# Down projection of an encoder: seven block products dealt anew over three phases, sums made in place

## The chip, the cores and the metric

The kernel runs on one core of a Trainium2 chip. A core has TensorE (PE: matrix products; PEld is its loading of weights), VectorE (DVE), ScalarE (ACT), GpSimd (POOL) and SyncE (SP, which here issues the DMAs). The metric is the device time of one execution in microseconds, lower is better; the time before is the median of three executions.

## The reference, cut to what matters

Two layers, 512 tokens, width 1024, all in float32. Each layer ends with the feed-forward part:

```python
h = rms_norm(x, pre_ffn_norm[l])
gate, up = jnp.split(jnp.einsum('bsd,df->bsf', h, ffn_w_gate_up[l]), 2, axis=-1)   # df: 2 x 2816
f = jnp.einsum('bsf,fd->bsd', jax.nn.silu(gate) * up, ffn_w_down[l])               # 2816 -> 1024
x = x + rms_norm(f, post_ffn_norm[l])
```

The change lies in the second product, f, which is called the down stage here.

## The kernel before

**Precision.** A float32 product is made of three: each operand is split into a high half (`A.activation(hi, src, Copy)`, written as fp32r by ACT) and a low half (`src - hi`, a subtraction on DVE or POOL), and `mm3` issues high by high, low by high, high by low into one PSUM bank. So each operand of the down stage costs one ACT and one DVE/POOL instruction of its width before PE can use it.

**The down stage (`down`).** The 2816 rows of the weight are 22 tiles of 128; tile k and tile k+11 are the two halves of the inner dimension (H = 11). Activations `act[k]` (a1) and `act[k+11]` (a2) are 128 x 512: columns q0 (tokens 0 to 255) and q1 (256 to 511). Weights are 128 x 1024: columns c0 and c1. With the blocks A11, A12 / A21, A22 of the activations and B11, B12 / B21, B22 of the weight, the 2 x 2 block product is made with seven products (a Strassen-Winograd form), each 11 steps of k with two banks (j = 0, 1) and three 128 x 512 matmuls in each: 66 matmuls.

- Phase 1 (`span(at, at + 56)`): four products m1, m5, m6, m7, 24 matmuls for each k. The names of PSUM are `ps_tp` (m1), `ps_mm` (m5), `ps_sc` (m6), `ps_av` and `ps_mm` (m7).
- Phase 2 (`span(at + 57, at + 85)`): two products, m2 and m3, in `ps_tp` and `ps_sc`, 12 matmuls for each k.
- Phase 3 (`span(at + 85, at + 99)`): one product m4 in `ps_mm`, 6 matmuls for each k, while the sums of the others are evacuated, normed and added to x (`post_half`, `finish`). In layer 0 `finish` also norms for the next layer and transposes (`ps_tp<-ident,p`).

Before, phase 1 reads tile k whole (r1, in `raw` or `tab`) and the right half of tile k+11 straight into `carry[k]`, which lies in the buffers `hT_h` and `hT_l`. Those hold the normed input that gate/up multiplies by, so they come free when gate/up's last product has read them. The sums of the Strassen form are made with subtractions (`sub(VG, ...)`) into `tmp`, `s`, `raw`, `carry` and `act`; VG lets the planner choose DVE or POOL.

**Gate/up (`ffn`)** makes act[f] for f = 0 to 21, from f = 2 on also in a Strassen form (`strassen`); the half act[f][:, 256:512] is written by POOL in the trace (`stk<-v` or `mix<-v`). One f takes PE 10.0 us.

**The order of the work.** The program records all operations, and `Program.run` plans them by a list: each has a priority by its place in the spans, costs and delays from a table in the code, and the planner writes one fixed order for each engine. An engine takes its instructions in that order; an instruction that waits holds up all behind it. Buffers: `raw` 2, `tab` 2, `whi` and `wlo` 4 each, `p` 3, `pT` 2, `s` 3, `tmp` 2, `stk` 18, `mix` 8. In layer 0 the norm weights of the next layer hold one of the two `tab` from phase 2 on. Every instruction has the one line L447 in the trace (L448 after), so tiles tell them apart. A split of weights reads `whi<-raw` on ACT and `wlo<-raw,whi` on DVE; one of activations `p<-stk` and `pT<-stk,p`.

Of the kernel before, what the change touches and what calls it, by code (L numbers as in the profile page):

```python
# [452 lines left out]
def encoder_kernel(  # L453
# [564 lines left out]
    def ffn(l, hT, at):  # L1018
# [120 lines left out]
        return act  # L1139

    def down(l, act, at):

# [54 lines left out]

        with pr.span(at + 56, at + 57):
            w1 = load_norm(l, 3, "v2")
            w2 = None if last else load_norm(l + 1, 0)  # L1200
# [4 lines left out]
            for j in range(2):
                u1, u2, u3, u5 = part_c[j]
                V.tensor_tensor(u3, m7[j], u2, ALU.add)
                V.tensor_tensor(u5, m5[j], u3, ALU.add)
                V.tensor_tensor(u2, m5[j], u2, ALU.add)
        with pr.span(at + 57, at + 85):  # L1210
            m2, m3 = ([bank(t), bank(t)] for t in ("tp", "sc"))
            for k in range(H):
# [8 lines left out]
                prod(m2, a, 0, w, c0, k)
                prod(m3, a, 256, w, c1, k)
        with pr.span(at + 85, at + 99):
            if not last:
# [4 lines left out]
            for j in range(2):
                u1, u2, u3, u5 = part_c[j]  # L1230
                for h, u, m in ((0, u1, m2[j]), (1, u2, m3[j])):
                    V.tensor_tensor(u, m, u, ALU.add)
                    post_half(ss[j], h, u, w1, u)
                finish(j, (u1, u2))
            tail = []
            for k in range(H):
                a1, a2 = act[k], act[k + H]
                w, a = (T("whi", F32R), T("wlo", F32R)), T("mix", F32R)
                a = a[:, q0], a[:, q1]
                split(w[0][:, c0], w[1][:, c0], a1, e=VG)  # L1240
                split(*a, a2[:, q1], e=VG)
                if k < H - 2:
                    prod(m4, a, 0, w, c0, k)
                else:
                    tail.append((a, w, k))
            for j in range(2):
# [2 lines left out]
                u3, u5 = part_c[j][2:]
                sub(V, u3, u3, m4[j])  # L1250
                post_half(ss[2 + j], 0, u3, w1, u3)
                finish(2 + j, (u3, u5))
# [117 lines left out]
```

## Time and profile before

| | us |
|---|---|
| median of 3 executions | 1298.52 (1298.27 to 1300.25) |
| profiled execution, its own time | 1296.75 |
| span of the trace | 1295.0 |
| PE busy / DVE busy / ACT busy / POOL busy in the span | 1230.5 / 1102.0 / 765.2 / 246.7 |
[...]

In a row of the timeline the numbers are start and duration in us, and in brackets the idle time of that engine just before and what ended it. Durations of neighbours overlap a little, so the price of an instruction in a full queue is the distance of two starts. A row of busy times by stretch reads: stretch, its length, busy us (and instructions) of PE, PEld, DVE, ACT and POOL, granted clock, DMA share, GB/s. Stretches used below: in layer 0 phase 1 runs from the end of gate/up at 523.49 to 592.79, phase 2 to 625.65, phase 3 to 650.58; in layer 1 from 1162.33 to 1231.51, 1265.91 and 1285.43, and the program ends 9.57 us later.

### The profile page before, as it was taken

The numbers are of one execution on the slowest core, as the hardware profiler recorded it, in microseconds if no ns is written. First come the engines' busy times: TensorE is split into PE (matmuls) and PEld (weight loads), VectorE is DVE, ScalarE is ACT, GpSimd is POOL, SyncE is SP. The second block draws the span as 40 slices with busy tenths as digits, with TensorE's granted clock in tenths as the row PEclk, the third lists the DMA queues.
The fourth block names the chain that finished last, engine by engine and source line by source line (L and its number), as shares of the span: only waits on it lengthen the run. The fifth ranks groups of instructions, "written<-read, shape, count | busy, mean of one in ns | idle before, by whom it ended". The sixth has DMA issues, their size and how long they took to land.

```text
span 1295.0 us, 20878 instructions
## 1 busy us (share of the span) xinstructions
PE 1230.5 (95%) x7608; PEld 1082.3 (84%) x7608; DVE 1102.0 (85%) x2147; ACT 765.2 (59%) x1515; POOL 246.7 (19%) x314
## 2 busy tenths in 40 slices
PE   7999999999999999999899999999999999998896
PEld 5787887888999999767677878878799999996674
DVE  5688889869888888999868797897798888889987
ACT  4675779755554455555646675796455544455553
POOL 1334423011011111001214353220201111110011
PEclk9999899999999999999899998999999999999999
DMA  6341232112333323524233321321233233325231
GB/s 223 113 144 60 70 100 80 33 50 98 114 98 113 116 99 98 175 80 138 72 112 121 121 70 50 111 62 50 67 98 113 98 100 119 109 84 185 77 119 66
DMA packets 42247, 129.68 MB, mean 100 GB/s; under 512 B 6048, under 2 KB 7072, under 8 KB 42144
## 3 DMA queue, kind: packets, MB, share of 16 engines
q1 hardware_dynamic: 42144, 128.35, 30.4%
q8 instruction: 60, 0.98, 0.3%
q14 instruction: 43, 0.35, 0.1%
HBM read 120.98 MB, written 2.10 MB: 95 GB/s over the span
## 4 chain that ended last, share of the span: by engine, by line
PE 69%; DVE 21%; ACT 3%; issue 3%; DMA 3%; POOL 1%; SPq 0%; DVEq 0%; POOLq 0%; ACTq 0%
PE ps_mm L447 39%; PE ps_sc L447 18%; PE ps_tp L447 9%; DVE wlo L447 6%; PE ps_av L447 4%; DVE pT L447 3%; DVE stk L447 2%; DVE v L447 2%; DVE tmp L447 1%; DVE s L447 1%; DMA raw<-in_wdn_dram 1%; ACT stk L447 1%; DVE tab L447 1%; ACT p L447 1%; DVE xs L447 1%
## 5 line engine op out<-in xcount | busy, mean ns | idle before, releaser
L447 ACT ACTIVATE whi<-raw 128x1024 fp32r<-128x1024 f32 (+2 forms) x186 | 180.2, 987 | 54.3 <-DMA raw<-in_wdn_dram 18.7
L447 DVE TENSOR_TENSOR wlo<-raw,whi 128x1024 fp32r<-128x1024 f32 (+2 forms) x171 | 192.1, 1139 | 19.9 <-ACT whi L447 19.2
L447 PE MATMUL ps_mm<-hT_h,whi 128*128 128x256 f32 (+1 forms) x352 | 114.6, 326 | 0.0
L447 PE MATMUL ps_mm<-hT_l,whi 128*128 128x256 f32 (+1 forms) x352 | 113.6, 323 | 0.3 <-DVE hT_l L447 0.3
L447 PE MATMUL ps_mm<-hT_h,wlo 128*128 128x256 f32 (+1 forms) x352 | 113.8, 323 | 0.1
L447 POOL TENSOR_TENSOR cb<-cb,mhalf 128x1 f32<-128x1 f32 (+3 forms) x52 | 54.5, 1052 | 237.0 <-DVE cb L447 234.5
L447 PE MATMUL ps_tp<-ident,p 128*128 128x128 f32 x608 | 87.2, 283 | 11.8 <-DVE p L447 11.7
L447 POOL TENSOR_TENSOR stk<-v 128x256 f32<-128x256 f32 x32 | 37.8, 1182 | 304.9 <-ACT v L447 264.4
L447 PE MATMUL ps_sc<-stk,stk 96*128 96x512 f32 (+2 forms) x320 | 92.6, 387 | 3.4 <-ACT p L447 2.5
L447 PEld LDWEIGHTS ps_tp<-ident,p 128*128 128x128 f32 x608 | 73.6, 146 | 22.4 <-DVE p L447 11.2
L447 DVE TENSOR_TENSOR pT<-ps_tp,pT 128x512 fp32r<-128x512 f32 (+1 forms) x128 | 79.0, 650 | 12.2 <-ACT pT L447 11.5
L447 ACT ACTIVATE pT<-ps_tp 128x512 fp32r<-128x512 f32 (+1 forms) x128 | 67.0, 567 | 26.7 <-PE ps_tp L447 25.8
L447 PE MATMUL ps_av<-pT,v 128*128 128x256 f32 x480 | 76.6, 289 | 6.1 <-DVE mix L447 3.5
L447 PEld LDWEIGHTS ps_av<-pT,v 128*128 128x128 f32 x480 | 69.1, 190 | 15.3 <-ACT pT L447 5.3
L447 ACT ACTIVATE v<-ps_mm 128x256 f32<-128x256 f32 (+3 forms) x72 | 26.6, 382 | 86.0 <-PE ps_mm L447 85.5
L447 PE MATMUL ps_mm<-whi,hT_h 128*128 128x512 f32 (+1 forms) x176 | 70.8, 402 | 1.5 <-DVE stk L447 1.0
L447 PEld LDWEIGHTS ps_mm<-hT_l,whi 128*128 128x128 f32 x352 | 66.4, 189 | 6.2 <-DVE hT_l L447 0.5
L447 PEld LDWEIGHTS ps_mm<-hT_h,wlo 128*128 128x128 f32 x352 | 66.5, 189 | 5.2 <-DVE wlo L447 0.3
L447 PEld LDWEIGHTS ps_mm<-hT_h,whi 128*128 128x128 f32 x352 | 66.5, 189 | 4.5
L447 PEld LDWEIGHTS ps_sc<-stk,stk 96*128 96x128 f32 (+2 forms) x320 | 52.3, 194 | 21.4 <-ACT p L447 5.3
L447 PE MATMUL ps_sc<-v,p 128*128 128x256 f32 x320 | 69.5, 280 | 0.0
L447 PE MATMUL ps_sc<-hT_h,wlo 128*128 128x256 f32 x224 | 64.4, 288 | 4.7 <-POOL wlo L447 4.7
(253 smaller groups left out, 3982.5 us busy)
## 6 DMA issues: line engine op xcount, KB each, us to landing
raw<-in_wgu_dram SPq DMA_DIRECT2D x48, 512.0 KB, 4.4
tab<-in_wgu_dram SPq DMA_DIRECT2D x40, 512.0 KB, 3.5
raw<-in_wdn_dram SPq DMA_DIRECT2D x28, 512.0 KB, 3.6
raw<-in_win_f_dram SPq DMA_DIRECT2D x16, 512.0 KB, 3.5
raw<-in_wo_dram SPq DMA_DIRECT2D x16, 512.0 KB, 3.5
tab<-in_wdn_dram SPq DMA_DIRECT2D x16, 512.0 KB, 3.4
raw<-in_win_g_dram SPq DMA_DIRECT2D x8, 512.0 KB, 3.7
tab<-in_natab_dram SPq DMA_DIRECT2D x8, 512.0 KB, 3.4
```

Of the source, the lines that this page charges most:

```text
L447: o.ins = getattr(self.issue[o.eng], method)(*[real(v) for v in a], **{k: real(v) for k, v in kw.items()}).ins
```

## The change

The seven products are kept, with other operands and in another distribution: phase 1 makes m1, m5, m6 and m2, phase 2 makes m7 and m3, phase 3 m4. Phase 1 reads both weight tiles whole, r1 into `raw` and r2 into `tab`, makes its sums in place in them and splits each 1024 wide; B of the last product is written to `carry[k]` as a plain difference, which nobody reads before phase 3. One sum of activations is made at the end of each gate/up step f >= 11, in place in act[f - 11], by two 256-wide operations. Phase 2 reads the two right halves again, as two loads of 256 KB, and makes one weight sum and two activation sums.

```diff
@@ ffn, after strassen(f)
+                if f >= H:
+                    a1, a2 = act[f - H], act[f]
+                    VG.tensor_tensor(a1[:, t1], a1[:, t1], a2[:, t1], ALU.add)
+                    VG.tensor_tensor(a1[:, t1], a1[:, t1], a1[:, t0], ALU.subtract)
@@ down, phase 1
-            m1, m5, m6 = ([bank(t), bank(t)] for t in ("tp", "mm", "sc"))
-            m7 = [bank("av"), bank("mm")]
+            m1, m6, m5 = ([bank(t), bank(t)] for t in ("tp", "sc", "mm"))
+            m2 = [bank("av"), bank("mm")]
             for k in range(H):
-                a1, a2, b22 = act[k], act[k + H], carry[k]
-                r1 = T(("raw", "raw", "tab", "tab")[k % 4])
+                a1, a2 = act[k], act[k + H]
+                r1, r2 = T("raw"), T("tab")
                 SP.dma_start(r1, wdn[l, k])
-                SP.dma_start(b22, wdn[l, k + H][:, c1])
-                t1, d = T("tmp"), T("s")
-                sub(VG, t1, r1[:, c1], r1[:, c0])
-                sub(VG, r1[:, c1], b22, r1[:, c1])
-                sub(VG, b22, b22, t1)
-                sub(VG, d[:, q0], a1[:, q0], a1[:, q1])
-                VG.tensor_tensor(d[:, q1], a1[:, q1], a2[:, q1], ALU.add)
-                sub(VG, a1[:, q1], d[:, q1], a1[:, q0])
+                SP.dma_start(r2, wdn[l, k + H])
+                d = T("s")[:, q0]
+                sub(VG, r1[:, c1], r1[:, c1], r1[:, c0])
+                sub(VG, r2[:, c1], r2[:, c1], r1[:, c1])
+                VG.tensor_tensor(d, a1[:, q1], a1[:, q0], ALU.add)
                 a = T("p", F32R), T("pT", F32R)
                 wa, wb = ((T("whi", F32R), T("wlo", F32R)) for _ in range(2))
-                for o, c, src in ((a, c0, a1), (wa, c0, r1[:, c0]), (a, c1, d), (wa, c1, t1), (wb, c0, b22),
-                                  (wb, c1, r1[:, c1])):
-                    split(o[0][:, c], o[1][:, c], src, e=VG)
-                sub(VG, a1[:, q0], a2[:, q0], a1[:, q1])
+                split(*wa, r1, e=VG)
+                split(a[0][:, 0:512], a[1][:, 0:512], a1, e=VG)
+                split(a[0][:, 512:768], a[1][:, 512:768], d, e=VG)
+                split(*wb, r2, e=VG)
+                split(a[0][:, 768:], a[1][:, 768:], a2[:, q0], e=VG)
+                sub(VG, carry[k], r2[:, c1], r2[:, c0])
...
@@ down, phase 2
-                r = T(("raw", "raw", "tab")[k % 3])
-                SP.dma_start(r, wdn[l, k + H])
+                r = T(("raw", "tab")[k % 2])
+                SP.dma_start(r[:, c0], wdn[l, k][:, c1])
+                SP.dma_start(r[:, c1], wdn[l, k + H][:, c1])
+                sub(VG, r[:, c0], r[:, c1], r[:, c0])
+                sub(VG, a2[:, q0], a2[:, q0], a1[:, q1])
+                sub(VG, a1[:, q1], a2[:, q1], a1[:, q1])
                 w, a = (T("whi", F32R), T("wlo", F32R)), (T("p", F32R), T("pT", F32R))
                 split(*w, r, e=VG)
-                split(a[0][:, q0], a[1][:, q0], a2[:, q0], e=VG)
-                split(a[0][:, q1], a[1][:, q1], a1[:, q0], e=VG)
-                sub(VG, a1, carry[k], r[:, c0])
+                split(a[0][:, q0], a[1][:, q0], a1[:, q1], e=VG)
+                split(a[0][:, q1], a[1][:, q1], a2[:, q0], e=VG)
...
```

The evacuation after phase 1 has five DVE operations where it had eight; the one after phase 2 has six where it had four.

What the planner makes of it on DVE, at three places. First, one steady step of phase 1 in layer 0. Before, twelve of the thirteen instructions of a step (a 128 x 512 `tmp<-tab` stands ahead of them):

```order
L447 TENSOR_TENSOR s_6700<-stk_4599 128x256
L447 TENSOR_TENSOR tab_6552<-hT_h_6431,tab_6552 128x512
L447 TENSOR_TENSOR s_6700<-stk_4599,stk_5952 128x256
L447 TENSOR_TENSOR hT_h_6431<-hT_h_6431,tmp_6693 128x512
L447 TENSOR_TENSOR stk_4599<-s_6700,stk_4599 128x256
L447 TENSOR_TENSOR wlo_6721<-tab_6552,whi_6640 128x512
L447 TENSOR_TENSOR pT_6727<-s_6700,p_6714 128x512
L447 TENSOR_TENSOR pT_6727<-stk_4599,p_6714 128x512
L447 TENSOR_TENSOR wlo_6721<-tmp_6693,whi_6640 128x512
L447 TENSOR_TENSOR wlo_6734<-hT_h_6431,whi_6711 128x512
L447 TENSOR_TENSOR wlo_6734<-tab_6552,whi_6711 128x512
L447 TENSOR_TENSOR stk_4599<-stk_5952,stk_4599 128x256
```

After, the whole step (raw is r1, tab is r2, the last row writes carry):

```order
L448 TENSOR_TENSOR raw_6610<-raw_6610 128x512
L448 TENSOR_TENSOR s_6680<-stk_4599 128x256
L448 TENSOR_TENSOR tab_6624<-tab_6624,raw_6610 128x512
L448 TENSOR_TENSOR pT_6688<-stk_4599,p_6629 128x512
L448 TENSOR_TENSOR wlo_6694<-raw_6610,whi_6685 128x1024
L448 TENSOR_TENSOR pT_6688<-s_6680,p_6629 128x256
L448 TENSOR_TENSOR wlo_6708<-tab_6624,whi_6696 128x1024
L448 TENSOR_TENSOR pT_6688<-stk_5964,p_6629 128x256
L448 TENSOR_TENSOR hT_h_6463<-tab_6624 128x512
```

Nine instructions stand where thirteen stood; four narrow splits of weights are two wide ones.

Second, phase 2 of layer 0 on DVE. Before, from one weight sum for phase 3 (`stk<-hT_h,raw`) to the next split but one:

```order
L447 TENSOR_TENSOR stk_4240<-hT_h_6431,raw_7031 128x512
L447 TENSOR_TENSOR wlo_7091<-raw_7050,whi_7080 128x1024
L447 TENSOR_TENSOR pT_7104<-stk_5706,p_7070 128x256
L447 TENSOR_TENSOR pT_7104<-stk_4365,p_7070 128x256
L447 TENSOR_TENSOR v_6968<-v_6968,v_6473 128x512
L447 TENSOR_TENSOR stk_4365<-hT_h_6431,raw_7050 128x512
L447 TENSOR_TENSOR wlo_7120<-tab_7078,whi_7110 128x1024
```

After, from the split of the weights of k = 4 (`raw`) and k = 3 (`tab`) to the sum for k = 5 (`tab`):

```order
L448 TENSOR_TENSOR wlo_7063<-raw_6961,whi_7043 128x1024
L448 TENSOR_TENSOR wlo_7068<-tab_7011,whi_7056 128x1024
L448 TENSOR_TENSOR pT_7073<-stk_4365,p_7065 128x256
L448 TENSOR_TENSOR pT_7073<-stk_5714,p_7065 128x256
L448 TENSOR_TENSOR stk_5839<-stk_5839,stk_4476 128x256
L448 TENSOR_TENSOR raw_7028<-raw_7028 128x512
L448 TENSOR_TENSOR stk_4476<-stk_5839,stk_4476 128x256
L448 TENSOR_TENSOR stk_5964<-stk_5964,stk_4599 128x256
L448 TENSOR_TENSOR mix_6089<-mix_6089,stk_4722 128x256
L448 TENSOR_TENSOR stk_4599<-stk_5964,stk_4599 128x256
L448 TENSOR_TENSOR wlo_7102<-raw_7028,whi_7093 128x1024
L448 TENSOR_TENSOR tab_7075<-tab_7075 128x512
```

The low half of the even k = 4 stands ahead of that of the odd k = 3, which PE multiplies first, and the sums of activations of later steps stand between.

Third, the beginning of phase 3 of layer 1 on DVE: `v<-ps_...` are evacuations, `xs<-v,cb,xs` the end of `finish`, `wlo<-stk` or `wlo<-hT_h` and `mix<-stk,mix` the low halves of m4's weights and activations. Before:

```order
L447 TENSOR_TENSOR v_14264<-ps_sc_14322,v_14264 128x512
L447 TENSOR_TENSOR v_14264<-v_14264,v_13778 128x512
L447 TENSOR_TENSOR v_14271<-v_14271,v_13778 128x512
L447 TENSOR_TENSOR v_14264<-v_14264,v_13778 128x512
L447 TENSOR_SCALAR cb_14612<-cb_14583 128x1
L447 TENSOR_TENSOR v_14271<-ps_sc_14328,v_14271 128x512
L447 TENSOR_TENSOR wlo_14622<-stk_11535,whi_14604 128x512
L447 SCALAR_TENSOR_TENSOR xs_117<-v_14264,cb_14620,xs_117 128x512 x2
L447 TENSOR_TENSOR v_14271<-v_14271,v_13778 128x512
L447 TENSOR_SCALAR cb_14651<-cb_14590 128x1
L447 TENSOR_TENSOR wlo_14653<-stk_11658,whi_14610 128x512
L447 TENSOR_TENSOR mix_14618<-stk_13011,mix_14618 128x256
```

After:

```order
L448 TENSOR_TENSOR v_14248<-ps_tp_14288,v_14248 128x512 x2
L448 TENSOR_TENSOR v_14232<-v_14232,v_13798 128x512
L448 TENSOR_SCALAR cb_14606<-cb_14295 128x1
L448 TENSOR_TENSOR v_14248<-ps_sc_14303,v_14248 128x512
L448 TENSOR_TENSOR v_14232<-v_14232,v_13798 128x512
L448 SCALAR_TENSOR_TENSOR xs_117<-v_14232,cb_14612,xs_117 128x512 x2
L448 TENSOR_TENSOR v_14248<-v_14248,v_13798 128x512
L448 TENSOR_SCALAR cb_14628<-cb_14308 128x1
L448 TENSOR_TENSOR v_14248<-v_14248,v_13798 128x512
L448 TENSOR_TENSOR wlo_14633<-hT_h_13766,whi_14559 128x512
L448 SCALAR_TENSOR_TENSOR xs_117<-v_14248,cb_14631,xs_117 128x512 x2
L448 TENSOR_TENSOR mix_13742<-stk_12769,mix_13742 128x256
```

The first low halves that DVE makes after the evacuations stand behind both `finish` operations. Ahead of them are ready: one weight split on DVE, and on POOL one weight and two activation splits, that is the operands of two of the eleven steps.

## Rows read from the trace of the kernel before

**Rows 1.** Busy times by stretch: phases 1 to 3 of both layers.
```profile
523.49:592.79 69.30, 63.75 (x255) 47.87 (x253) 68.79 (x129) 36.99 (x67) 2.52 (x4) 0.98 0.40 134
592.79:625.65 32.86, 30.84 (x134) 24.70 (x132) 31.29 (x52) 19.84 (x36) 5.35 (x6) 1.00 0.49 159
625.65:650.58 24.93, 20.21 (x84) 15.78 (x82) 22.46 (x40) 16.39 (x37) 7.13 (x8) 0.86 0.10 25
1162.33:1231.51 69.18, 62.35 (x254) 46.62 (x253) 68.73 (x129) 37.79 (x67) 2.51 (x4) 1.00 0.39 133
1231.51:1265.91 34.40, 31.82 (x133) 24.33 (x132) 31.05 (x48) 17.25 (x33) 5.02 (x6) 1.00 0.33 107
1265.91:1285.43 19.52, 16.15 (x67) 11.97 (x65) 16.15 (x31) 9.81 (x24) 1.81 (x2) 1.00 0.15 55
```

**Rows 2.** Timeline of PE, phase 1 of layer 0.
```profile
566.31 0.50 PE L447 MATMUL ps_tp<-whi,p 128*128 128x512 f32 x1 [0.36 <-ACT p L447]
...
567.65 0.39 PE L447 MATMUL ps_tp<-whi,p 128*128 128x512 f32 x1
...
572.28 0.39 PE L447 MATMUL ps_mm<-wlo,p 128*128 128x512 f32 x1
...
573.07 0.50 PE L447 MATMUL ps_tp<-whi,p 128*128 128x512 f32 x1 [0.40 <-ACT p L447]
```

**Rows 3.** Timeline of DVE: one phase 1 step, and a wide split.
```profile
566.35 0.68 DVE L447 TENSOR_TENSOR pT<-stk,p 128x512 fp32r<-128x512 f32 x1
566.95 0.68 DVE L447 TENSOR_TENSOR wlo<-tmp,whi 128x512 fp32r<-128x512 f32 x1
...
568.76 0.41 DVE L447 TENSOR_TENSOR stk<-mix,stk 128x256 f32<-128x256 f32 x1
569.09 0.68 DVE L447 TENSOR_TENSOR tmp<-raw 128x512 f32<-128x512 f32 x1
...
1244.31 1.22 DVE L447 TENSOR_TENSOR wlo<-raw,whi 128x1024 fp32r<-128x1024 f32 x1
1245.45 0.75 DVE L447 TENSOR_TENSOR pT<-stk,p 128x256 fp32r<-128x256 f32 x2
```

**Rows 4.** Timeline of PE where gate/up ends, layer 0 and layer 1.
```profile
527.71 0.50 PE L447 MATMUL ps_av<-whi,p 128*128 128x512 f32 x1 [1.25 <-ACT whi L447]
...
529.09 0.77 PE L447 MATMUL ps_av<-wlo,p 128*128 128x512 f32 x1 [0.65 <-DVE wlo L447]
...
531.36 0.63 PE L447 MATMUL ps_sc<-whi,pT 128*128 128x512 f32 x1
531.79 0.63 PE L447 MATMUL ps_sc<-wlo,p 128*128 128x512 f32 x1
...
1166.56 0.50 PE L447 MATMUL ps_av<-whi,p 128*128 128x512 f32 x1 [1.29 <-ACT whi L447]
```

**Rows 5.** Busy times by stretch, just behind that place in layer 0.
```profile
530.00:533.00 3.00, 3.00 (x9) 2.33 (x8) 3.00 (x6) 1.46 (x3) 0.00 (x0) 0.57 1.01 378
533.00:536.00 3.00, 3.00 (x15) 2.43 (x14) 2.66 (x5) 2.72 (x5) 0.00 (x0) 1.00 1.03 409
```

**Rows 6.** Timeline, one gate/up step of layer 0: DVE and POOL.
```profile
452.40 0.69 DVE L447 TENSOR_TENSOR tmp<-tab,s 128x512 fp32r<-128x512 f32 x1 [1.20 <-PE ps_mm L447]
...
455.12 1.18 POOL L447 TENSOR_TENSOR stk<-v 128x256 f32<-128x256 f32 x1 [8.84 <-ACT v L447]
```

**Rows 7.** DMA issues: KB each, median us from issue to landing.
```profile
raw<-in_wdn_dram SPq DMA_DIRECT2D x28, 512.0 KB, 3.6
...
hT_l<-in_wdn_dram SPq DMA_DIRECT2D x6, 256.0 KB, 6.3
```

**Rows 8.** Timeline of PE: step 1 of phase 2, and the first transposes, layer 0.
```profile
598.22 0.50 PE L447 MATMUL ps_tp<-wlo,p 128*128 128x512 f32 x1 [2.02 <-DVE wlo L447]
...
636.67 1.97 PE L447 MATMUL ps_tp<-ident,p 128*128 128x128 f32 x8 [1.91 <-DVE p L447]
```

**Rows 9.** Timeline of DVE and PE, phase 3 of layer 1.
```profile
1271.28 1.40 DVE L447 SCALAR_TENSOR_TENSOR xs<-v,cb,xs 128x512 f32<-128x512 f32 x2
1272.61 0.68 DVE L447 TENSOR_TENSOR v<-v,v 128x512 f32<-128x512 f32 x1
...
1274.39 0.50 PE L447 MATMUL ps_mm<-whi,mix 128*128 128x512 f32 x1 [1.53 <-DVE mix L447]
```

More of the change, by code (lines that the diff above doesn't have):

```diff
@@ L24 @@
 NF = 2816 // P
+H = NF // 2
 CH = 1024
@@ L1160, in down @@
         with pr.span(at, at + 56):
-            m1, m5, m6 = ([bank(t), bank(t)] for t in ("tp", "mm", "sc"))
-            m7 = [bank("av"), bank("mm")]
+            m1, m6, m5 = ([bank(t), bank(t)] for t in ("tp", "sc", "mm"))
+            m2 = [bank("av"), bank("mm")]
             for k in range(H):
-                a1, a2, b22 = act[k], act[k + H], carry[k]
-                r1 = T(("raw", "raw", "tab", "tab")[k % 4])
+                a1, a2 = act[k], act[k + H]
+                r1, r2 = T("raw"), T("tab")
                 SP.dma_start(r1, wdn[l, k])
-                SP.dma_start(b22, wdn[l, k + H][:, c1])
-                t1, d = T("tmp"), T("s")
-                sub(VG, t1, r1[:, c1], r1[:, c0])
-                sub(VG, r1[:, c1], b22, r1[:, c1])
-                sub(VG, b22, b22, t1)
-                sub(VG, d[:, q0], a1[:, q0], a1[:, q1])
-                VG.tensor_tensor(d[:, q1], a1[:, q1], a2[:, q1], ALU.add)
-                sub(VG, a1[:, q1], d[:, q1], a1[:, q0])
+                SP.dma_start(r2, wdn[l, k + H])
[3 more added lines that the diff above has]
+                VG.tensor_tensor(d, a1[:, q1], a1[:, q0], ALU.add)
                 a = T("p", F32R), T("pT", F32R)
                 wa, wb = ((T("whi", F32R), T("wlo", F32R)) for _ in range(2))
-                for o, c, src in ((a, c0, a1), (wa, c0, r1[:, c0]), (a, c1, d), (wa, c1, t1), (wb, c0, b22),
-                                  (wb, c1, r1[:, c1])):
-                    split(o[0][:, c], o[1][:, c], src, e=VG)
-                sub(VG, a1[:, q0], a2[:, q0], a1[:, q1])
+                split(*wa, r1, e=VG)
[4 more added lines that the diff above has]
+                sub(VG, carry[k], r2[:, c1], r2[:, c0])
                 prod(m1, a, 0, wa, c0, k)
-                prod(m5, a, 768, wa, c1, k)
-                prod(m6, a, 256, wb, c0, k)
-                prod(m7, a, 512, wb, c1, k)
+                prod(m5, a, 512, wa, c1, k)
+                prod(m6, a, 256, wb, c1, k)
+                prod(m2, a, 768, wb, c0, k)
         hT = None
@@ L1206, in down @@
                 u1, u2, u3, u5 = part_c[j]
-                V.tensor_tensor(u3, m7[j], u2, ALU.add)
-                V.tensor_tensor(u5, m5[j], u3, ALU.add)
-                V.tensor_tensor(u2, m5[j], u2, ALU.add)
+                V.tensor_tensor(u3, m5[j], u2, ALU.add)
+                V.tensor_tensor(u1, m2[j], u1, ALU.add)
         with pr.span(at + 57, at + 85):
-            m2, m3 = ([bank(t), bank(t)] for t in ("tp", "sc"))
+            m7, m3 = ([bank(t), bank(t)] for t in ("tp", "sc"))
             for k in range(H):
                 a1, a2 = act[k], act[k + H]
-                r = T(("raw", "raw", "tab")[k % 3])
-                SP.dma_start(r, wdn[l, k + H])
+                r = T(("raw", "tab")[k % 2])
[4 more added lines that the diff above has]
+                sub(VG, a1[:, q1], a2[:, q1], a1[:, q1])
                 w, a = (T("whi", F32R), T("wlo", F32R)), (T("p", F32R), T("pT", F32R))
                 split(*w, r, e=VG)
-                split(a[0][:, q0], a[1][:, q0], a2[:, q0], e=VG)
-                split(a[0][:, q1], a[1][:, q1], a1[:, q0], e=VG)
-                sub(VG, a1, carry[k], r[:, c0])
-                prod(m2, a, 0, w, c0, k)
+                split(a[0][:, q0], a[1][:, q0], a1[:, q1], e=VG)
+                split(a[0][:, q1], a[1][:, q1], a2[:, q0], e=VG)
+                prod(m7, a, 0, w, c0, k)
                 prod(m3, a, 256, w, c1, k)
@@ L1227, in down @@
             for j in range(2):
-                post_half(ss[2 + j], 1, part_c[j][3], w1, part_c[j][3])
+                post_half(ss[j], 0, part_c[j][0], w1, part_c[j][0])
             for j in range(2):
                 u1, u2, u3, u5 = part_c[j]
[L1231 to L1234, printed above, removed]
+                V.tensor_tensor(u5, m7[j], u3, ALU.add)
+                V.tensor_tensor(u2, m7[j], u2, ALU.add)
+                V.tensor_tensor(u3, m3[j], u3, ALU.add)
+                post_half(ss[j], 1, u3, w1, u3)
+                finish(j, (u1, u3))
+            for j in range(2):
+                post_half(ss[2 + j], 1, part_c[j][3], w1, part_c[j][3])
             tail = []
             for k in range(H):
-                a1, a2 = act[k], act[k + H]
+                a2 = act[k + H]
                 w, a = (T("whi", F32R), T("wlo", F32R)), T("mix", F32R)
                 a = a[:, q0], a[:, q1]
-                split(w[0][:, c0], w[1][:, c0], a1, e=VG)
+                split(w[0][:, c0], w[1][:, c0], carry[k], e=VG)
                 split(*a, a2[:, q1], e=VG)
@@ L1248, in down @@
                     part(m4, j, a, 0, w, c0, k)
[L1249 to L1252, printed above, removed]
+                u2, u5 = part_c[j][1], part_c[j][3]
+                sub(V, u2, u2, m4[j])
+                post_half(ss[2 + j], 0, u2, w1, u2)
+                finish(2 + j, (u2, u5))
         return hT
```

1 line of the change is left out of this document (removed).

## The prediction

> **What bounds the kernel now.** I read the busy times by stretch first. In phase 1 DVE is busy 68.79 of 69.30 us in layer 0 and 68.73 of 69.18 in layer 1, PE only some 63 [rows 1]. The timelines say the same per step. On PE, 20 matmuls in a row stand 0.232 us apart (567.65 to 572.28), so the 24 of a step need 5.57; but a step lasts 6.76 (566.31 to 573.07) [rows 2]. On DVE a 512-wide subtraction takes 0.60 from start to start, a 256-wide one 0.33 and a 1024-wide one 1.14 [rows 3]: nine of the first and four of the second make 6.72. So phase 1 goes at DVE's pace, and PE idles about 1.2 in each step.
>
> Three other places matter. Where gate/up ends, PE stands still for 1.25 and 0.65 in layer 0 and 1.29 in layer 1 [rows 4]: the weights of the first steps were loaded into buffers that gate/up had only just left. [...] Phase 2 lasts 32.86 and 34.40 against 132 x 0.232 = 30.6 of PE; phase 3 lasts 24.93 and 19.52 against 15.3 [rows 1]. In phase 3 of layer 0 PE waits for DVE before the transposes [rows 8], in layer 1 for the first low halves of m4 [rows 9].
>
> **Phase 1.** Thirteen DVE instructions become nine: four 512-wide, two 1024-wide, three 256-wide, 2.40 + 2.28 + 0.99 = 5.67. PE's 5.57 is now almost the same, and it decides how much DVE has done ahead. The order puts 12 of phase 1's 264 matmuls ahead of gate/up's last one, so PE has 252 left, 58.5. Behind gate/up's last row, DVE has 80 rows of phase 1 left: 28 256-wide, 35 512-wide, 17 1024-wide, 9.2 + 21.0 + 19.4 = 49.6. DVE thus starts with steps 0 and 1 prepared and loses 0.1 in each step, about one of the lead. Carry is no longer loaded and its write has no reader before phase 3, so the pause at gate/up's end goes too. I take 58.5 + 0.5 = 59.0: **-10.3 in layer 0, -10.2 in layer 1**.
>
> The loads grow to 1.05 MB in each 5.57 us, 188 GB/s; 378 and 409 were moved around 533 [rows 5]. A buffer of `raw` or `tab` is held some 4.7 of the 11.1 us in which it must come round; 6.4 are left, against 3.6 for 512 KB alone and 6.3 for the crowded 256 KB [rows 7]. I take the first as nearer, nothing waits; at 6.9 a step would be about 5.8, which is +2.2 per layer.
>
> **Gate/up.** From f = 11 on each step gets two 256-wide additions, 0.66. PE paces the step (10.0); DVE waits 1.20 for PE in one place [rows 6] and some 0.2 elsewhere, which hides them. They follow POOL's product of 1.18 [rows 6], which had time until phase 1. I take nothing; the bound above is rival E.
>
> **Phase 2.** On DVE a step was one 1024-wide, one 512-wide and two 256-wide, 2.40; now two more 256-wide, 3.06, against 2.78 for PE's 12 matmuls. So DVE paces it. In layer 0 there is only one free `tab`, and the order puts the split of an even k (`raw`) ahead of the odd k before it, which PE takes first: the low half that is late is always the odd one. Five evacuations (3.0) and 10 x 1.14 + 11 x 0.60 + 38 x 0.33 = 30.5 stand ahead of the end of the weights' split of k = 9, at 33.5 after the phase began. PE then has 22 matmuls, six of them already m4's: 5.1, so 38.6 against 32.86, **+5.7**. In layer 1 both `tab` are there. Behind an equal burst of 3.0 stand 28.4 to the last low half, 31.4, and ten matmuls behind it, 33.7 against 34.40: **-0.7**. PE's stalls in layer 0 are four of 1.5 to 2, like the 2.02 of before [rows 8].
>
> **Phase 3.** Layer 0: 1.4 of m4 is done early, and the chain from phase 2's end to the transposes is 9.7 by the same prices where it was 11.0 (636.67 less 625.65 [rows 1, 8]); 22.5 against 24.93, **-2.4**. Layer 1: operands for two of m4's eleven steps are ready (one weight split on DVE, one step on POOL). All other low halves stand on DVE behind six evacuations, four norm products and the two `finish` operations of 1.33 each [rows 9], 11.1 in all. The queue begins when the first bank of m7 is full, at 31.9, so the next operand comes at 43.0. PE is done with the two steps at 33.7 + 2.8 = 36.5 and idles 6.5. Then come 53 matmuls, 12.3, and something for the clock. A stretch at half rate costs 0.43 less 0.23 for each matmul [rows 4]; before, the 1.53 there [rows 9] cost no clock and the pause at 527 did [rows 4, 5], so I take half of 13 such matmuls, 1.3. That makes 43.0 + 13.6 - 33.7 = 22.9, **+3.4**.
>
> **The sum.** Layer 0: -10.3 + 5.7 - 2.4 = -7.0. Layer 1: -10.2 - 0.7 + 3.4 = -7.5. Together -14.5. The profiled execution lasted 1296.75, the median is 1298.52: 1282.3 profiled, **1284.0** as a median.
>
> **Rivals.**
>
> **B, the wide operations cost more.** My prices are distances in a full queue. By the durations of the same rows (0.68, 0.41, 1.22 [rows 3]) the 80 rows of phase 1 take 56.0, still under 58.5; phase 2's 30.5 become 35.3, so +4.8 per layer: 1293.6. Against it: the four kinds follow each other at the short distances all through phase 1, and the old step sums up by them; for it: many of the new ones read what the instruction ahead has just written. [...]
>
> **C, less is given back.** DVE's 49.6 leave 8.9 of PE's 58.5 in phase 1. I let it use little of them, since the weights of phase 2 must wait for `raw` and `tab`. If it gets as far ahead as in phase 1, the late splits of layer 0 cost nothing (5.7 back), and the queue in phase 3 of layer 1 begins earlier (half of 3.4 back): 1284.0 - 7.4 = 1276.6. For it speaks that phase 1 needs both buffers of each kind itself only up to its last step; against it the order, in which the odd splits stand late.
>
> **D, slower: the clock.** If PE's pauses of 1.5 to 2 in phase 2 bring the granted clock to half as the one at 527 did, the 132 matmuls of phase 2 take 56.8 at 0.43 where I have 38.6 and 33.7, and phase 3 some 6 more: about +25 per layer, 1334. It decides from 14.5 / 0.2 = 73 matmuls at half rate that no wait hides. For it stands the stretch of 530 to 533 [rows 5]; against it 1166.56 [rows 4] and 598.22 [rows 8], pauses of 1.29 and 2.02, in phases with a mean of 1.00 [rows 1]. [...]
>
> **E, slower: gate/up loses its cover.** If DVE waits in each step for POOL's product, 0.66 + 1.18 less the slack of 1.4 is 0.44 in each of 22 steps, +9.7: 1293.7. With the cover wholly gone it is 1.84 x 22 = 40.5 and 1324.5; it is slower than before from 0.66 in each step.
>
> **F, no change.** That the narrow splits stay is excluded by the order. Gains and stalls would have to cancel by chance.
>
> **Chances.** A, this sum, 0.58: its own range is 1280 to 1289 (loads +4.4; the clock of phase 3 and a stall more or less). B 0.17, C 0.15, D 0.04, E 0.04 (half of it slower than before), F 0.02. Within 0.2%, 2.6 us, a measurement of this kernel can't tell a change. Range: 1276.5 (C within) to 1293 (most of B within); outside are D, E, F and the edge of B and C, about 0.2. Faster 0.91, same 0.03, slower 0.06.
>
> **What the profile after would show.** If I am right: phase 1 of 59 in both layers with PE spaced 0.232 throughout and DVE idling now and then; no pause at gate/up's end and no drop of the clock at 530; gate/up steps still 10.0; in phase 2 of layer 0 waits of PE for `wlo` on odd k only; in layer 1 a pause of 6 us on PE behind the first two steps of phase 3, ended by DVE's `mix` or `wlo`. Phase 1 over 61 with PE waiting for ACT or DVE refutes the count of DVE, waiting for a DMA that of the buffers; a clock under 0.9 in phase 2 means D; gate/up steps over 10.2 mean E. Wrong most easily is the sum for phases 2 and 3, which depends on how far DVE is ahead when phase 1 ends.

## The result, and the profile after

The changed kernel takes **1284.57 us** (median of 4 runs, 1282.41 to 1287.61) where the one before takes 1298.68: ratio 0.9891, 95% interval 0.9878 to 0.9904, 14.1 us faster. The profiled execution took 1285.56. The busy times by stretch, which answer to [rows 1] (phases 1, 2 and 3 of layer 0, then of layer 1):

```profile
525.68:584.14 58.46, 58.03 (x252) 46.68 (x251) 58.42 (x95) 32.18 (x51) 2.93 (x3) 1.00 0.60 192
584.14:623.75 39.61, 35.03 (x140) 26.55 (x138) 37.60 (x75) 20.97 (x40) 3.51 (x5) 0.96 0.44 141
623.75:647.26 23.51, 19.20 (x77) 14.76 (x76) 21.71 (x40) 15.37 (x35) 5.58 (x5) 0.85 0.08 23
1160.03:1217.93 57.90, 57.90 (x252) 46.71 (x250) 57.82 (x95) 32.44 (x51) 3.93 (x3) 1.00 0.61 194
1217.93:1250.84 32.91, 31.85 (x133) 24.31 (x132) 32.91 (x62) 19.00 (x35) 3.15 (x6) 1.00 0.33 107
1250.84:1274.46 23.62, 17.48 (x67) 13.27 (x65) 17.72 (x34) 9.75 (x24) 4.01 (x4) 0.86 0.12 45
```

| stretch | before | after | change | forecast |
|---|---|---|---|---|
| layer 0: phase 1, 2, 3 | 69.30, 32.86, 24.93 | 58.46, 39.61, 23.51 | -10.84, +6.75, -1.42 | -10.3, +5.7, -2.4 |
| layer 1: phase 1, 2, 3 | 69.18, 34.40, 19.52 | 57.90, 32.91, 23.62 | -11.28, -1.49, +4.10 | -10.2, -0.7, +3.4 |

The six changes add up to -14.2. The one profiled execution is only 11.2 faster than that of before (1296.75); 3.2 were lost ahead of the two down stages and 0.2 won at the end. Layer 0's gate/up ends at 525.68 instead of 523.49, and the way from the end of layer 0 to the end of layer 1's gate/up is 1.0 longer (512.77 instead of 511.75). In each layer 0.7 of that is work moved forward: 15 matmuls of phase 1 now stand ahead of gate/up's last one, 12 before. For the other 1.8 no run here shows a cause.

In phase 1 PE and DVE are both busy all the time, within a few tenths. A step on DVE in the timeline (answers to [rows 3]):

```profile
549.99 0.68 DVE L448 TENSOR_TENSOR hT_h<-tab 128x512 f32<-128x512 f32 x1
550.59 0.69 DVE L448 TENSOR_TENSOR raw<-raw 128x512 f32<-128x512 f32 x1
...
551.52 0.69 DVE L448 TENSOR_TENSOR tab<-tab,raw 128x512 f32<-128x512 f32 x1
...
554.20 1.22 DVE L448 TENSOR_TENSOR wlo<-tab,whi 128x1024 fp32r<-128x1024 f32 x1
555.34 0.42 DVE L448 TENSOR_TENSOR pT<-stk,p 128x256 fp32r<-128x256 f32 x1
555.67 0.68 DVE L448 TENSOR_TENSOR hT_h<-tab 128x512 f32<-128x512 f32 x1
```

From 549.99 to 555.67 are 5.68; the forecast was 5.67. The chained operations, each reading what the one ahead wrote, cost no more than the old ones.

In gate/up, the timeline of POOL (its product ends each step) and DVE, answering to [rows 6]:

```profile
446.11 1.18 POOL L448 TENSOR_TENSOR stk<-v 128x256 f32<-128x256 f32 x1 [8.85 <-ACT v L448]
456.13 1.18 POOL L448 TENSOR_TENSOR stk<-v 128x256 f32<-128x256 f32 x1 [8.84 <-ACT v L448]
...
457.79 0.41 DVE L448 TENSOR_TENSOR stk<-stk,stk 128x256 f32<-128x256 f32 x1
463.43 0.69 DVE L448 TENSOR_TENSOR tmp<-tab,s 128x512 fp32r<-128x512 f32 x1 [0.81 <-PE ps_mm L448]
```

Steps still 10.0 apart, the two additions in their places (the second at 458.46), and DVE's wait for PE down from 1.20 to 0.81: the cover held and is not used up.

In phase 2 of layer 0 PE waits at odd k (1, 3 and 5), as forecast, though at three places and not at four, and once for ACT's `whi`. Its timeline, with the DVE row behind the longest of these waits:

```profile
587.83 0.50 PE L448 MATMUL ps_tp<-wlo,p 128*128 128x512 f32 x1 [0.28 <-DVE wlo L448]
595.46 0.50 PE L448 MATMUL ps_tp<-wlo,p 128*128 128x512 f32 x1 [1.46 <-DVE wlo L448]
595.79 0.40 PE L448 MATMUL ps_tp<-whi,p 128*128 128x512 f32 x1
596.03 0.40 PE L448 MATMUL ps_tp<-whi,pT 128*128 128x512 f32 x1
...
602.63 0.50 PE L448 MATMUL ps_tp<-whi,p 128*128 128x512 f32 x1 [1.83 <-ACT whi L448]
604.29 0.50 PE L448 MATMUL ps_tp<-wlo,p 128*128 128x512 f32 x1 [0.93 <-DVE wlo L448]
...
600.80 0.69 DVE L448 TENSOR_TENSOR tab<-tab 128x512 f32<-128x512 f32 x1 [1.31 <-DMA tab<-in_wdn_dram]
```

And two stretches of 3 and 5 us behind the pauses, the granted clock third from the end:

```profile
606.00:609.00 3.00, 3.00 (x9) 2.32 (x9) 2.91 (x7) 0.79 (x3) 0.00 (x0) 0.55 0.80 236
637.00:642.00 5.00, 5.00 (x13) 3.66 (x14) 4.93 (x12) 2.58 (x5) 0.00 (x0) 0.50 0.00 0
```

One wait is DVE's own for the load into the single free `tab`: the slot was late, not only the split. Behind the double pause of 1.83 and 0.93 the clock falls to half for some 3 us, and again in phase 3; behind the single one of 1.46 the matmuls stay 0.24 apart (595.79 to 596.03).

In phase 3 of layer 1, PE and the DVE rows that it waits for:

```profile
1253.87 0.40 PE L448 MATMUL ps_mm<-whi,mix 128*128 128x512 f32 x1
1260.41 0.80 PE L448 MATMUL ps_mm<-whi,mix 128*128 128x512 f32 x1 [6.14 <-DVE mix L448]
...
1257.47 0.69 DVE L448 TENSOR_TENSOR wlo<-hT_h,whi 128x512 fp32r<-128x512 f32 x1
1258.61 1.41 DVE L448 SCALAR_TENSOR_TENSOR xs<-v,cb,xs 128x512 f32<-128x512 f32 x2 [0.45 <-POOL cb L448]
1259.94 0.42 DVE L448 TENSOR_TENSOR mix<-stk,mix 128x256 fp32r<-128x256 f32 x1
```

A pause of 6.14, ended by the first `mix`, which stands behind the second `finish` (a `wlo` stands ahead of it), 42.0 us after phase 2 began; the forecast had 6.5 and 43.0.

### The profile page after: what moved, and what is told of

It reads as the page before. It is cut to its first block, busy times and chain, and to the rows that moved or that the text cites. A ratio compares the mean times of both kernels' runs of the same rounds, so it can differ in the third digit from the quotient of the medians.

```text
span 1283.8 us, 20910 instructions
## 1 busy us (share of the span) xinstructions
PE 1228.7 (96%) x7608; PEld 1086.4 (85%) x7608; DVE 1103.3 (86%) x2152; ACT 761.1 (59%) x1493; POOL 249.1 (19%) x309
## 4 chain that ended last, share of the span: by engine, by line
PE 78%; DVE 13%; DMA 3%; ACT 3%; issue 2%; POOL 1%; SPq 0%; DVEq 0%; POOLq 0%; ACTq 0%
PE ps_mm L448 42%; PE ps_sc L448 20%; PE ps_tp L448 11%; PE ps_av L448 5%; DVE wlo L448 2%; DVE pT L448 2%; DVE v L448 2%; DVE stk L448 2%; DMA raw<-in_wgu_dram 1%; DVE raw L448 1%; ACT stk L448 1%; DMA raw<-in_wdn_dram 1%; DVE xs L448 1%; DVE tmp L448 1%; DVE tab L448 1%
## 5 line engine op out<-in xcount | busy, mean ns | idle before, releaser
L448 DVE TENSOR_TENSOR wlo<-raw,whi 128x1024 fp32r<-128x1024 f32 (+1 forms) x165 | 198.1, 1217 | 18.6 <-ACT whi L448 18.0
L448 ACT ACTIVATE whi<-raw 128x1024 fp32r<-128x1024 f32 (+1 forms) x180 | 184.3, 1042 | 39.4 <-PE ps_mm L448 10.2
L448 PE MATMUL ps_tp<-ident,p 128*128 128x128 f32 x608 | 86.8, 281 | 10.6 <-DVE p L448 10.4
```

The costliest lines, as they stand in the source:

```text
L448: o.ins = getattr(self.issue[o.eng], method)(*[real(v) for v in a], **{k: real(v) for k, v in kw.items()}).ins
```

## The experiments

The kernel before ran beside every group (medians 1299.5 to 1299.6), so the medians stand side by side.

**The changed kernel again.**

> The changed kernel as it is, beside the other runs of this group. All theories: 1284 to 1286, phase 1 near 58 in both layers.

1285.66, ratio 0.9905 (0.989 to 0.992), phase 1 of 58.77 and 57.89. The runs below are compared with this one. In phase 2 of layer 0 its clock goes another way than in the first profile. PE's timeline:

```profile
595.80 0.50 PE L448 MATMUL ps_tp<-wlo,p 128*128 128x512 f32 x1 [1.45 <-DVE wlo L448]
596.41 0.63 PE L448 MATMUL ps_tp<-whi,pT 128*128 128x512 f32 x1
596.84 0.63 PE L448 MATMUL ps_tp<-wlo,p 128*128 128x512 f32 x1
...
605.12 0.51 PE L448 MATMUL ps_tp<-wlo,p 128*128 128x512 f32 x1 [0.92 <-DVE wlo L448]
```

The same single pause, 1.45 at 595.80, is here followed by matmuls 0.43 apart until 599.4, the distance that goes with the clock of 0.55 in the first profile (606.22 to 606.65 there); behind the double pause (0.77 at 603.47, then 0.92) they stand 0.23 apart (605.47 to 605.70).

**What a phase 1 step costs on DVE: three doses.** First, the activation sum back in phase 1:

```diff
@@ ffn
-                if f >= H:
-                    a1, a2 = act[f - H], act[f]
-                    VG.tensor_tensor(a1[:, t1], a1[:, t1], a2[:, t1], ALU.add)
-                    VG.tensor_tensor(a1[:, t1], a1[:, t1], a1[:, t0], ALU.subtract)
@@ down, phase 1
-                d = T("s")[:, q0]
+                dd = T("s")
+                d = dd[:, q0]
+                VG.tensor_tensor(dd[:, q1], a1[:, q1], a2[:, q1], ALU.add)
+                sub(VG, a1[:, q1], dd[:, q1], a1[:, q0])
```

> The activation sum a1 is made in phase 1 again, through a buffer of s, as the kernel before did, and no longer during gate/up; all else as changed. Behind gate/up's last instruction DVE then has 56.4 us of phase 1 ahead of the first evacuation, by the distances 0.33, 0.60 and 1.14; the changed kernel has 52.3, the one before 64.2. Theory (DVE's lead covers phase 1): 56.4 is still less than PE's 58.5, so phase 1 stays within 1 us of 58.5 and 57.9, and what is lost is lead for phase 2: 0 to 4 us per layer, about 1288. Rival (DVE's step of 6.33 paces phase 1): phase 1 of 64 in both layers, about 1296. Rival (where the sum is made is worth nothing): 1284.6.

Second, narrow splits of weights:

```diff
-                split(*wa, r1, e=VG)
+                for c in (c0, c1):
+                    split(wa[0][:, c], wa[1][:, c], r1[:, c], e=VG)
...
-                split(*wb, r2, e=VG)
+                for c in (c1, c0):
+                    split(wb[0][:, c], wb[1][:, c], r2[:, c], e=VG)
```

> In phase 1 each 1024-wide split of weights is made as two 512-wide ones again, on ACT and DVE; all else as changed. DVE has 54.9 us behind gate/up instead of 52.3. Theory (covered by PE's 58.5): phase 1 as in the changed kernel, the time within 2 us of it, 1284.6 to 1286.6. Rival (the wide low halves are what makes phase 1 shorter): PE waits for wlo in each step, phase 1 over 62 in both layers, 1292 or more.

Third, work of no use:

```diff
-                sub(VG, carry[k], r2[:, c1], r2[:, c0])
+                for _ in range(2):
+                    sub(V, carry[k], r2[:, c1], r2[:, c0])
```

> In each step of phase 1 the difference that goes to carry is written twice on DVE, one idle 512-wide operation of 0.60 that nothing waits for; all else as changed. DVE has 56.8 us behind gate/up instead of 52.3. Theory (DVE's amount behind gate/up plus some 5 sets phase 1 as soon as that is more than 58.5; the run with the sum in phase 1 had 56.4 and 61.6): phase 1 of 62 in both layers, phase 2 up to 2.8 longer, about 1296. Rival (the sum in phase 1 cost time by its buffer of s and its place, not by DVE's amount): phase 1 under 59, 1285 to 1287.

Medians 1297.9 (ratio to before 0.999, 0.9979 to 1.0), 1289.97 (0.9931, 0.9918 to 0.9945) and 1298.35 (0.9995, 0.9984 to 1.0006). The stretches of phases 1 and 2 of layer 0, one fence for each kernel in that order:

```profile
527.02:588.58 61.56, 60.55 (x255) 46.91 (x253) 61.42 (x107) 33.43 (x52) 3.70 (x5) 1.00 0.55 180
588.58:631.02 42.44, 36.61 (x133) 27.44 (x132) 39.29 (x76) 21.87 (x38) 3.74 (x4) 0.88 0.43 135
```

```profile
524.65:583.87 59.22, 59.22 (x257) 47.87 (x256) 59.21 (x113) 36.56 (x72) 2.64 (x4) 1.00 0.57 187
583.87:625.73 41.86, 36.27 (x139) 27.46 (x138) 39.13 (x76) 21.43 (x40) 3.71 (x4) 0.92 0.42 137
```

```profile
526.93:589.95 63.02, 59.93 (x251) 46.15 (x250) 62.33 (x101) 32.35 (x48) 2.27 (x4) 1.00 0.52 171
589.95:633.31 43.36, 36.85 (x140) 27.67 (x139) 40.84 (x80) 23.00 (x42) 3.96 (x5) 0.92 0.42 139
```

And PE in phase 1 with one more operation (first row), and behind phase 1 with narrow splits (second row):

```profile
565.64 0.50 PE L448 MATMUL ps_tp<-whi,pT 128*128 128x512 f32 x1 [0.47 <-DVE pT L448]
...
587.42 0.50 PE L448 MATMUL ps_tp<-wlo,p 128*128 128x512 f32 x1 [2.92 <-DVE wlo L448]
```

| kernel | DVE from gate/up's last row to the first evacuation | PE's matmuls left in phase 1, at 0.232 | phase 1, layers 0 and 1 | phase 2, layers 0 and 1 |
|---|---|---|---|---|
| before | 64.2 | 252, 58.5 | 69.30, 69.18 | (other products) |
| one more operation | 56.8 | 249, 57.8 | 63.02, 61.61 | 43.36, 36.38 |
| sum in phase 1 | 56.4 | 252, 58.5 | 61.56, 61.62 | 42.44, 35.68 |
| narrow splits | 54.9 | 255, 59.2 | 59.22, 59.14 | 41.86, 35.00 |
| changed | 52.3 | 249, 57.8 | 58.46, 57.90 | 39.61, 32.91 |

The second column counts rows of the order at 0.33, 0.60 and 1.14, the third the matmuls of phase 1 that stand behind gate/up's last one. With narrow splits PE is busy for all of the 59.22: the phase lasts as long as its 255 matmuls, so DVE's 54.9 is still covered in it, as that run's theory had it. With 56.4 and 56.8 it is not: PE waits for DVE's `pT`, in the run with the sum in the last four steps of layer 0, in the one with one more operation from 546 on in every step, and phase 1 is 3.1 and 3.8 to 5.2 longer than PE's own amount. So the theory of the first run, that 56.4 is covered by 58.5, is wrong; its rival's time came (1296), but not its phase of 64. The third run, forecast as DVE's amount and some 5, came near in phase 1 (62 forecast, and 1296 for the whole). That 5 is not PE's last step, as the forecast of the next experiment has it. In the changed kernel, layer 0, DVE comes to these rows 3.9 us behind gate/up's end, since it still works for gate/up, needs 52.8 for them, and starts the first evacuation 1.8 ahead of the end of phase 1: 58.5 (in layer 1 3.2, 52.8 and 1.9).

What is covered isn't free. Phase 2, which DVE paces too, now starts without DVE's lead: in layer 0 PE waits there 2.51 to 2.92 for the first late `wlo`, where the changed kernel has 0.28, and the phase is 2.1 to 3.8 longer in each layer of all three runs. That is where the narrow splits lose their time (forecast for the whole kernel within 2 us, measured 4.3). An operation of 0.60 that nothing waits for, once in a step, thus costs 12.7 us, nearly the whole gain; the sum made during gate/up is worth 12.2, the wide splits 4.3. The last two add up to more than the gain of 13.9: they are no shares of it.

**The pause at gate/up's end, taken out of the kernel before.**

```diff
                 SP.dma_start(r1, wdn[l, k])
+                if k < 2:
+                    b22 = T("tab")[:, c0]
                 SP.dma_start(b22, wdn[l, k + H][:, c1])
...
+                if k < 2:
+                    A.activation(carry[k], b22, AF.Copy)
```

> The kernel before, with one edit: for k = 0 and 1 the right half of tile k+11 is loaded into a buffer of tab and ACT copies the finished block to carry, so that the first two steps wait for no buffer that gate/up still holds. Behind gate/up's last instruction DVE has 62.5 us of work instead of 64.2. Theory (phase 1 of before is DVE's work behind gate/up plus some 5 for PE's last step, as 64.2 and 69.3 were): the pauses of 1.25 and 1.29 and the half clock go, yet phase 1 falls by 1.7 alone, to 67.5, about -3.5 in all. Rival (the pause itself is time that the change wins): PE gains 1.9 and 2.3 and the clock's 2.5 besides, -6 or more in all.

1299.13, ratio 1.0004 (0.9992 to 1.0016). PE's pauses at 527 and 1166 are gone and the clock stays at 1.00, yet phase 1 is as long as before (69.56 in layer 0, 69.18 in layer 1; 255 of its matmuls stand in it instead of 252, which is 0.7):

```profile
525.20:594.76 69.56, 63.48 (x257) 47.14 (x256) 67.15 (x128) 37.58 (x68) 3.23 (x5) 1.00 0.39 134
```

Its timeline of DVE where the pause had been:

```profile
531.63 0.69 DVE L447 TENSOR_TENSOR tmp<-tab 128x512 f32<-128x512 f32 x1 [1.37 <-DMA tab<-in_wdn_dram]
536.96 0.69 DVE L447 TENSOR_TENSOR wlo<-hT_h,whi 128x512 fp32r<-128x512 f32 x1 [1.02 <-ACT whi L447]
```

DVE is busy 67.15 instead of 68.79, as expected, but now waits itself, 1.37 and 1.02, for the next loads (the second time by way of ACT's `whi`), and even the expected 3.5 did not come. So taking PE's pause away won nothing by itself: DVE, busy or waiting, sets the end of the phase. What it would be worth without DVE's new waits, this run doesn't show.

**Where phases 2 and 3 give back.** The norm weights out of `tab`:

```diff
...
-            w2 = None if last else load_norm(l + 1, 0)
+            w2 = [] if not last else None
+            for h, sl in (halves() if not last else ()):
+                w2.append(T("tmp"))
+                SP.dma_start(w2[h], nrm[l + 1, 0][:, sl])
```

> The norm weights of the next layer lie in the two buffers of tmp, which the down stage no longer uses, so that both buffers of tab serve phase 2 of layer 0 too. Theory (the late odd steps of phase 2 in layer 0 come from the one free tab): phase 2 of layer 0 falls from 39.6 to about 33, the waits for wlo and whi at odd k and the half clock behind them go, phase 3 gives back at most 1.5: about 1279. Rival (the amount of DVE's work bounds that phase): phase 2 stays over 38, 1284.6.

The post work of the first two tiles (the `post_half` calls, the evacuations and `finish`) later in the list, in layer 1:

```diff
+            with pr.span(at + 85 + (13 if last else 0), at + 85 + (13 if last else 0)):
+                for j in range(2):
+                    post_half(ss[j], 0, part_c[j][0], w1, part_c[j][0])
...
```

> In layer 1 alone, the evacuation, norm products and finish of the first two token tiles are put behind the low halves of m4 in the list. Theory (the pause of 6.14 in phase 3 of layer 1 is DVE's order): the pause goes and the clock stays at 1.00 there, the last matmul comes 7 to 8 us earlier; DVE still has some 19.5 us for a phase in which PE needs 15.3, so that about 4 come back behind the last matmul: about 1281. Rival (m4's operands wait for something else, ACT or a buffer): the pause stays, 1284.6. Rival (the work put off is as long at the end as the pause was): no pause, and 1284 to 1286.

Both, with `13 if last else 5`:

> Both edits that worked on one stage together: the next norm weights in tmp (phase 2 of layer 0 at 33) and the post work of the first two tiles later in the list, in layer 1 behind m4's low halves and in layer 0 behind those of the first four to six steps. Theory (in phase 3 of layer 0 too PE waits because the norm work stands ahead of the low halves): layer 1 as in the run with the post work later, phase 3 of 15.3; in layer 0 phase 3 falls from 28.4 to about 23, as DVE has some 22 us for it; in all about 1271. Rival (phases 2 and 3 of layer 0 together are bound by DVE's amount): phase 3 of layer 0 stays at 27 or more, about 1275.

And with `13 if last else 8`:

> As the run with both edits, but the post work of layer 0 stands some three steps of m4 later in the list. Theory (in layer 0 low halves and norm work share one DVE that is busy 23.7 of 24.1 us there, so their order can win little more): within 1.5 us of 1272.8. Rival (PE still waits for low halves behind norm work): phase 3 of layer 0 falls to 22 or less, 1270.

Medians 1285.24 (ratio 0.9889, 0.9874 to 0.9904), 1275.65 (0.982, 0.9807 to 0.9834), **1272.76 (0.9806, 0.9793 to 0.982)** and 1273.8 (0.9797, 0.978 to 0.9813). Phases 2 and 3 of layer 0 in the first of these runs:

```profile
583.09:616.10 33.01, 31.82 (x133) 24.30 (x132) 33.01 (x62) 18.79 (x34) 3.26 (x6) 1.00 0.50 168
616.10:644.53 28.43, 22.66 (x83) 17.11 (x82) 24.81 (x45) 16.45 (x37) 7.12 (x7) 0.76 0.06 18
```

Phase 3 of layer 1 and what lies behind it, in the second:

```profile
1247.04:1262.35 15.31, 15.31 (x67) 12.21 (x65) 15.31 (x32) 9.58 (x24) 1.86 (x2) 1.00 0.05 17
1262.35:1273.50 11.15, 0.16 (x1) 0.00 (x0) 7.58 (x13) 1.31 (x4) 2.82 (x4) 0.70 0.45 167
```

Phase 3 of both layers in the third:

```profile
618.22:642.32 24.10, 20.84 (x83) 15.87 (x82) 23.66 (x44) 16.67 (x37) 5.39 (x6) 0.86 0.03 5
1246.30:1261.59 15.29, 15.29 (x67) 12.21 (x65) 15.29 (x32) 9.57 (x24) 1.85 (x2) 1.00 0.05 16
```

The first shows a repaired stage and an unmoved time. Phase 2 of layer 0 falls by 6.6 to 33.01, so the one free `tab` was its cause, and phase 3 takes 4.9 back where 1.5 was allowed for (28.43, clock 0.76): as in the changed kernel, m4's next low halves stand behind norm work on DVE, and PE waits for `mix` 3.36 at 622.90 and 1.78 at 630.20. The second shows that this is order: with the same instructions the pause of 6.14 is gone, the clock is 1.00, phase 3 is 8.3 shorter, and of the work put off only 1.8 comes back at the end (11.15 against 9.34 from 1274.46 to 1283.8 in the changed kernel; 4 was expected). That is 6.5 of the 10.0 between the medians; in the profile phase 3 also begins 3.8 earlier (1247.04 instead of 1250.84), ahead of the place of the edit, for which no run here shows a cause. Together they give the fastest kernel here, 12.9 under the changed one. In its phase 3 of layer 0 DVE is busy 23.66 of 24.10, and a later place for the post work (the fourth run) wins no more, which speaks for amount and not order in what remains there.

**Carry's difference on POOL**, on top of both:

```diff
-                sub(VG, carry[k], r2[:, c1], r2[:, c0])
+                sub(G, carry[k], r2[:, c1], r2[:, c0])
```

> As the run with both edits, and the difference that goes to carry is written by POOL in phase 1, 11 operations of 512 columns per layer. DVE has 46.6 us behind gate/up. Theory (PE paces phase 1, and what DVE saves there is lead for phase 2 as far as buffers let it): phase 1 stays near 58, phase 2 of both layers falls from 33.0 and 33.2 towards PE's 30.6, by 1 to 2 each, about 1269 to 1271. Rival (POOL's operations hold DVE up while they run): the 512-wide operations of DVE stand further apart than 0.60 there, and the time is 1273 or more.

> The same kernel as the run with carry on POOL, for a profile of an undisturbed execution; it took 1294.6, 22 more than without the edit. Theory now (DVE stands still, or each of its operations takes longer, while POOL's 512-wide subtraction of 1.27 runs, and the buffer of tab is held until POOL is done): DVE's busy time in phase 1 grows by up to 11 x 1.27 = 14 per layer less the 6.6 it saved, and phase 1 is 63 to 67. Rival (only the buffers): DVE idles in phase 1, waiting for a DMA into tab, and its 512-wide distances stay 0.60.

1294.58 (ratio 0.996, 0.9946 to 0.9975) and 1294.74 (0.9964, 0.9953 to 0.9975): 22 slower than without the edit. The rows are from the second. Phase 1 of layer 0:

```profile
525.67:590.71 65.04, 61.10 (x252) 48.29 (x251) 57.35 (x82) 32.35 (x49) 39.48 (x13) 0.95 0.52 169
```

The timelines of POOL, the DMA queue and DVE in it:

```profile
532.73 1.42 POOL L448 TENSOR_TENSOR hT_h<-tab 128x512 f32<-128x512 f32 x1 [4.04 <-DVE tab L448]
542.79 2.27 POOL L448 TENSOR_TENSOR hT_h<-tab 128x512 f32<-128x512 f32 x1 [4.24 <-DVE tab L448]
548.44 10.64 POOL L448 TENSOR_TENSOR hT_h<-tab 128x512 f32<-128x512 f32 x1 [3.38 <-DVE tab L448]
...
559.10 0.33 SPq L448 DMA_DIRECT2D tab<-in_wdn_dram  x1
...
543.83 1.51 DVE L448 TENSOR_TENSOR pT<-s,p 128x256 fp32r<-128x256 f32 x1
...
556.91 0.68 DVE L448 TENSOR_TENSOR raw<-raw 128x512 f32<-128x512 f32 x1
557.51 0.41 DVE L448 TENSOR_TENSOR s<-stk 128x256 f32<-128x256 f32 x1
562.84 0.69 DVE L448 TENSOR_TENSOR tab<-tab,raw 128x512 f32<-128x512 f32 x1 [4.92 <-DMA tab<-in_wdn_dram]
```

The length of phase 1, 65.04, is what the theory of the second run said, and its mechanism is half of it. Where POOL comes through between two operations of DVE, the second of them is held up: at 542.79 POOL takes 2.27, and DVE's 256-wide operation at 543.83 takes 1.51 instead of 0.41. So is the 1024-wide one at 564.05, with 2.30 instead of 1.21. DVE is busy for 57.35 in this phase where the run with both edits has 58.66, so that most of the 6.6 that the edit took off DVE came back. Where DVE's queue goes on instead, its operations stand 0.60 apart as ever (556.91 to 557.51) and POOL waits: an operation that took 1.42 at 532.73 lasts 10.64 from 548.44 on and ends 1.2 after DVE's last one. Till then it holds its `tab`, the next load is issued at 559.10, and DVE waits 4.92 for it; its waits in the phase add up to 7.7. So both came, the theory's longer operations and the rival's buffer, the latter by way of POOL's late turn.

## Why the prediction was right, and where it was not

- **Phase 1** (-10.3, -10.2; measured -10.84, -11.28). Right: nine instructions of 5.68 in place of thirteen, and PE paces it. What failed is the margin. I set DVE's 49.6 against PE's 58.5 and found 8.9 free. But DVE comes to these rows 3.9 and 3.2 us behind gate/up's end and has 52.3 of rows ahead of the first evacuation, so it was busy for 58.42 of 58.46 us; the idling now and then that I forecast did not come. By the doses DVE's rows are covered where they are 4.3 less than PE's own amount (54.9 and 59.2) and not where they are 2.1 less (56.4 and 58.5). In the changed kernel they are 5.5 less (52.3 and 57.8), so its cover is 1.2 to 3.4, and what is covered is paid in phase 2. The 58.5 itself was a slip, since 252 is the count of matmuls left in the kernel before; in the changed one 249 are left, 57.8, and the 0.7 between them stands in gate/up. By the same token the 56.0 of rival B, which is 6.4 more than 49.6, would not have been covered: the runs with 56.4 and 56.8, 4.1 and 4.5 more than 52.3, lost 3 to 5 in phase 1.
- **The pause at gate/up's end** went, as forecast, with carry's loads, and no clock was lost there (1.00 in each stretch of 3 us from 527 to 536). Taken out of the kernel before it won nothing; the sum had counted it inside phase 1, where DVE's amount was the time.
- **The loads**: 192 and 194 GB/s in phase 1, and no wait for a DMA in it. In phase 2 of layer 0 there is one, 1.31, at the single `tab`.
- **Gate/up** (0): right, steps of 10.0, the 0.7 of moved work in each layer apart. Rival E did not come.
- **Phase 2** (+5.7, -0.7; measured +6.75, -1.49). The mechanism of layer 0 was right, as the run with a free `tab` shows; the term was 1.1 too small. Its stalls were not four of 1.5 to 2 but 0.28, 1.46, and 1.83 with 0.93 behind it. The clock behind that double pause was not in it: eight matmuls from 605.37 to 608.74 take 3.37 instead of 1.86, which is 1.5.
- **Phase 3** (-2.4, +3.4; measured -1.42, +4.10). Right in sign and place. In layer 0 the parts given (1.4 of m4, 1.3 of the chain) make 2.7 and not 2.4; the chain took 8.8 where 9.7 was forecast, and a wait of 2.63 and a half clock behind it (637 to 642) were not in the sum. In layer 1 the pause came as computed (6.14 for 6.5), and a loss of clock with it: the mean of the phase is 0.86, and the eight matmuls from 1260.41 to 1263.99 take 3.58 instead of 1.86, 1.7 where the sum had 1.3 (half of 13 matmuls, a count that was my estimate). The 11.1 of DVE's queue there is more than its named parts at their prices (6 x 0.60, 4 x 0.60, 2 x 1.33, 8.7 in all); measured were 10.4, from 1249.91 to 1260.36, with a weight split, small operations and a wait of 0.45 between them.
- **Rival B** is out: the steady step is 5.68 by distances of starts. The durations of its rows are, to 0.01, those that B reckoned with, 0.69, 0.42 and 1.22 for the three widths (550.59, 555.34 and 554.20 above), but the starts are closer (0.60, 0.33 and 1.14), and the starts set the time here.
- **Rival C** is out: the lead that it would have used did not exist, since DVE had no idle time in phase 1.
- **Rival D** has its mechanism, not its size: the clock did fall behind the double pause in phase 2 and behind those of phase 3, in phase 2 for the eight matmuls above and in phase 3 of each layer to means of 0.85 and 0.86. It would have had to fall for 73 matmuls. Nor did a pause's length tell here whether the clock falls: in the changed kernel run again the single pause at the same place halved it and the double one did not. Of the waits of phase 2, one was followed by half the clock in each of the two executions (1.83 with 0.93 in the first, 1.45 in the second), the others were not.

That 1284.0 came so near to 1284.57 is partly luck: the errors of the six terms, from -1.1 to +1.1, cancel, and the profiled execution, forecast at 1282.3, took 1285.56, as the 3.2 lost ahead of the down stages were in no term.
